# Two-layer mixture of experts on one core: whole expert products, other tile addresses, a rearranged router tail and a loop in another place

## The chip, the cores and the metric

One core of a Trainium2 chip runs the kernel. The metric is the device time of one execution in microseconds (us). The engines are TensorE (PE, with PEld for its weight loads), VectorE (DVE), ScalarE (ACT), GpSimd (POOL) and SyncE (SP, which issues the transfers). The line numbers (L911) are those of the kernel before.

## The reference

All is float32, 512 tokens of width 1024. Two layers of one kind come first, then a third block of another kind and a feed-forward layer. A layer of the first kind is

```python
h = rmsnorm(x, g_mix[i]);  u = h @ w_in[i]
...
x = x + merged @ w_o[i]
x = x + hierarchical_moe(rmsnorm(x, g_ffn[i]), ...)
ple_gate = jax.nn.sigmoid(rmsnorm(x, g_ple[i]) @ w_ple_gate[i])
x = x + (p[i] @ w_ple[i]) * ple_gate
```

with `merged` from a stick-breaking and a differential attention. The mixture has 4 groups of 8 experts. A token takes the best group by its group logits and in it the best 2 experts; each expert is `(silu(x @ w_gate) * (x @ w_up)) @ w_down` with a hidden width of 256, and its rows are weighted by the token's gates and added up. The third block has a dilated window attention, a gated linear recurrence and a block-sparse attention with a relative bias.

## The kernel before, in words

**Products.** Most float32 matmuls are made of three with rounded operands: an operand is split in a high part (`copyH`, L227 on ACT) and a low rest (`subL`, L240 on DVE or POOL), and `mm3` (L272 to L274) multiplies high by high, high by low and low by high. In the trace "out<-a,b" of a matmul names the moving operand a first and the stationary operand b second: `mm<-f,wh` is the feature-major projection `proj_f`, 512 columns of f against a 128x128 piece of a weight tile wh; `mm<-wh,q` is `add_out` (L639), the output projection, with 256 weight columns moving; `proj_v` (L484) has 256 weight columns moving too. Weights come by SP into `raw` tiles (4 of 4 KB per partition) and are cut into `wh` tiles (6). Tiles of one tag share a ring of buffers; `q` has 12, `o` 8, and `tmp`, `g`, `f16` belong to the phase "mix" (7, 4 and 2 buffers), `X`, `wu`, `gs`, `hid`, `y` and another `g` (4) to the phase "moe", whose memory is the same.

**Router.** `add_out` adds an output tile to x (L651) by 256 columns c and 128 tokens tt and calls `router.then(c, tt)`. That queues a transpose of x (L755), its split in high and low (L760 on ACT, L761 on DVE) and the products with the router's weights. Behind the last c of a token tile it forms the norm at once: a square on ACT (L333), the reciprocal root on DVE (L310 to L318), a scaled copy of 128x1024 on DVE (L345), the high part on ACT and the low part of 128x1024 on POOL (L240). These eight tiles `hs` fill the `o` ring. `moe_route` copies the logits (L808 on ACT), transposes them (L811) and runs the routing chain on DVE, from L814 to L903: best group, best two experts, gates, each token's place in the sorted rows.

**Experts.** The sorted rows stand in 17 groups g of two experts with 64 rows each (the last one has one). Tokens are gathered by products with one-hot tiles (`gather_oh`, L993 and L994 on DVE; `gather_rows` on PE, copied to X by ACT and DVE in turn). The up product multiplies 64 rows of two experts side by side, in the two halves of the array's columns: 8 pairs of matmuls of 64 stationary and 512 moving columns (`mm<-wu,X` and the same with raw, wh or q in place of wu). The down product has 4 pairs (`z<-wh,hid`, `z<-raw,hid`). Between them lie `gate`, `hidden` (transposes L1056), `rows` (the split of the result), `back` (transposes of the one-hot tile, L1036) and `combine` (`o<-q,g`, added to x by L1078 on DVE). An order written out by hand, for PE, ACT, DVE and POOL, interleaves all this: a list of steps, each one pair of matmuls of a product, and tables (`GAT`, `BAT`, `CAT`, `HT`) that say between which steps the other work goes. A weight's buffer is loaded again when the step that reads it last has been written.

**Ahead and behind.** A loop (`moe_overflow`, L1200 and L1202) for experts with more than 64 rows stands between the routing chain and the first gather. Its trip count is read from memory by every engine; with the inputs here it makes no turn, and all engines meet at it. Behind the steps the last groups' rows are combined (`z<-q,g`, added by L1179). Then come the norm of the next part and the p input's product: `ple_rows` (transposes L1289, `mm<-wh,o`, copies L1303) and the gate product. Outside the hand-written order a scheduler picks instructions by priority, so parts of `ple_rows` run among the last steps. Its tiles (p, its transposes and its results) are from the `o` ring too.

Of the kernel before, what the change touches and what calls it, by code (L numbers as in the profile page):

```python
# [18 lines left out]
S, D = 512, 1024  # L19
# [88 lines left out]
class Kern:  # L108
    def __init__(self, ctx, tc, A, out, dbg=None, stop=None):
# [7 lines left out]
        self.ph = None  # L117
# [4 lines left out]
    PHASES = {"mix": dict(tmp=7, g=4, f16=2, reset=1), "moe": dict(y=1, gs=2, g=4, X=2, hid=2, wu=NWU)}  # L122

    def phase(self, name):
# [6 lines left out]
        self.phbufs = dict(self.PHASES[name])  # L131

    def ring(self, tag, shape, dt):

        return self.t(tag, shape, dt, bufs={"raw": RAW, "wh": WHL}[tag])
# [106 lines left out]
    def wload(self, src, a, b, eH="act", eL="dve"):  # L242
# [4 lines left out]
        return self.wcut(raw, a, b, eH, eL)  # L247
# [5 lines left out]
    def wcut(self, raw, a, b, eH="act", eL="dve"):  # L253

        h, l = (self.ring("wh", [128, a, b], F32R) for _ in range(2))
# [236 lines left out]
    def proj_f_halves(self, hT, w, c0, r):  # L492

        r += [self.mmps([128, S]) for _ in range(2)]
        wc = [self.wload(self.wk(w, c0, kh), 4, 256) for kh in range(2)]
# [230 lines left out]
    def router(self, l, xs):  # L726
# [18 lines left out]
        self.routed = lt, r, hs  # L745
# [23 lines left out]
        def then(c, tt):  # L769
# [18 lines left out]
        return then  # L788

    def moe_route(self, l, xs):  # L790
# [3 lines left out]
        lt, r, hs = self.routed  # L794
# [13 lines left out]
        nc.scalar.copy(ls, lt)  # L808
# [94 lines left out]
        v.tensor_sub(GHL[:, :, 1], d, GHL[:, :, 0].bitcast(F32))  # L903
# [4 lines left out]
    def moe(self, l, xs):  # L908
# [9 lines left out]
        for g, tags in ((0, ("raw", "raw", "wh", "wh")), (1, ("q",) * 4)):  # L918
            for c in range(4):
                for i in range(2):  # L920
                    t = self.t(tags[c], [128, 2, 2, 256], F32, bufs={"raw": RAW, "wh": WHL, "q": 12}[tags[c]])
# [936 lines left out]
```

## Time and profile before

| | |
|---|---|
| median of 3 runs | 2855.8 us (2852.76 to 2857.8) |
| the profiled execution | 2855.61 us, span 2853.9 us |
| PE, PEld busy | 2691.7 (94%), 1995.1 (70%) |
| DVE, ACT, POOL busy | 1379.6 (48%), 973.3 (34%), 313.8 (11%) |
| DMA | 383.56 MB, 134 GB/s in the mean |
| granted clock of PE, mean | 0.968 |

The span is the time from the first to the last instruction; some 2 us lie around it. The expert stages are 504 to 845 us in the first layer and 1408 to 1751 us in the second. A row of a timeline has the start, the duration, engine, line, operation and tiles, and behind "x" how many were put together; where several stand in a row the duration goes to the end of the last. PE's ends are modelled and overlap the next start, so the pace of matmuls is read from start to start.

### The profile page before, as it was taken

To read this page: it belongs to the slowest core of one execution; us is meant where nothing else is said; L and a number is where in the kernel's file an instruction comes from. 1 tells how busy PE (TensorE), PEld (TensorE's weight loads), DVE (VectorE), ACT (ScalarE), POOL (GpSimd) and SP (SyncE) were. 2 spreads that over 40 slices of the span, in tenths; PEclk is the share of its full clock that TensorE was granted. 3 is DMA by queue.
4 is the path that set the end of the run, shared out by engine and by line. 5 is a ranking of instruction groups with operands and counts; after the bars stand their busy time and mean duration, and the time that the engine had idled before them with its cause. 6 is when DMAs were issued, how large, how long until landed. Compare 5 with 4: busy or idle time off the path is not lost.

```text
span 2853.9 us, 37149 instructions
## 1 busy us (share of the span) xinstructions
PE 2691.7 (94%) x14711; PEld 1995.1 (70%) x14711; DVE 1379.6 (48%) x2585; ACT 973.3 (34%) x1756; POOL 313.8 (11%) x346
## 2 busy tenths in 40 slices
PE   7899996999999989999699999899999899999998
PEld 6777785544548777788444545878776677877798
DVE  6677536233247567643633335754345812533323
ACT  4555322111124455532211113544453532322222
POOL 0221001000000022010100000210001533011101
PEclk9999997999999989999799999999999999999999
DMA  5112234788853211233778883322212233223322
GB/s 171 45 45 67 84 119 149 287 304 292 289 203 98 77 52 47 65 92 116 238 290 283 290 308 104 111 82 64 65 51 70 77 104 108 86 92 96 96 86 71
DMA packets 224770, 383.56 MB, mean 134 GB/s; under 512 B 19658, under 2 KB 162599, under 8 KB 224592
## 3 DMA queue, kind: packets, MB, share of 16 engines
q1 hardware_dynamic: 224592, 381.13, 39.8%
q8 instruction: 118, 1.93, 0.3%
q14 instruction: 60, 0.49, 0.1%
HBM read 374.23 MB, written 6.85 MB: 134 GB/s over the span
## 4 chain that ended last, share of the span: by engine, by line
PE 43%; DVE 5%; ACT 1%; POOL 1%; issue 1%; POOLq 0%; DVEq 0%; ACTq 0%
PE mm L272 8%; PE mm L274 8%; PE mm L273 7%; PE z L911 5%; PE mm L911 4%; PE o L911 2%; PE z L272 1%; PE z L274 1%; PE z L273 1%; DVE tmp L345 1%; PE o L524 1%; PE o L1440 1%; PE mm L484 0%; DVE tmp L1606 0%; PE z L1429 0%
## 5 line engine op out<-in xcount | busy, mean ns | idle before, releaser
L240 DVE TENSOR_TENSOR wh<-raw,wh 128x1024 fp32r<-128x1024 f32 (+1 forms) x251 | 304.1, 1214 | 474.2 <-ACT wh L227 471.9
L272 PE MATMUL mm<-f,wh 128*128 128x512 f32 x1296 | 519.0, 402 | 5.1 <-DVE q L238 2.3
L273 PE MATMUL mm<-f,wh 128*128 128x512 f32 x1296 | 518.8, 400 | 0.0
L274 PE MATMUL mm<-f,wh 128*128 128x512 f32 x1296 | 517.6, 400 | 0.1
L227 ACT ACTIVATE wh<-raw 128x1024 fp32r<-128x1024 f32 (+1 forms) x278 | 290.4, 1046 | 485.3 <-PE mm L273 331.8
L272 PEld LDWEIGHTS mm<-f,wh 128*128 128x128 f32 x1296 | 244.6, 189 | 71.1 <-issue 6.8
L274 PEld LDWEIGHTS mm<-f,wh 128*128 128x128 f32 x1296 | 244.9, 189 | 57.7 <-issue 2.1
L273 PEld LDWEIGHTS mm<-f,wh 128*128 128x128 f32 x1296 | 245.1, 189 | 55.5 <-issue 1.7
L911 PE MATMUL mm<-wu,X 128*64 128x512 f32 x928 | 229.2, 606 | 0.0
L911 PEld LDWEIGHTS z<-g,o 128*128 128x128 f32 x1152 | 141.6, 193 | 51.0 <-issue 14.6
L911 PE MATMUL z<-g,o 128*128 128x256 f32 (+1 forms) x1152 | 154.7, 289 | 10.8 <-DVE g L994 10.8
L911 PEld LDWEIGHTS o<-q,g 128*128 128x128 f32 x448 | 75.4, 188 | 104.4 <-issue 56.8
L484 PE MATMUL mm<-wh,f 128*128 128x256 f32 x960 | 138.4, 298 | 5.4 <-ACT f L386 3.1
L911 PE MATMUL o<-q,g 128*128 128x512 f32 x448 | 134.7, 422 | 3.3 <-DVE q L1078 3.3
L484 PEld LDWEIGHTS mm<-wh,f 128*128 128x128 f32 x960 | 128.1, 201 | 10.9 <-ACT f L386 4.8
L1078 DVE TENSOR_TENSOR q<-q,o 128x512 f32<-128x512 f32 x112 | 76.6, 684 | 108.7 <-PE o L911 108.7
L911 PEld LDWEIGHTS mm<-wu,X 128*64 128x64 f32 x928 | 55.5, 136 | 87.3 <-issue 79.2
L272 PE MATMUL mm<-wh,q 128*128 128x256 f32 x384 | 112.1, 292 | 3.7 <-ACT q L227 3.7
L274 PE MATMUL mm<-wh,q 128*128 128x256 f32 x384 | 110.1, 287 | 2.4 <-POOL q L240 2.2
L273 PE MATMUL mm<-wh,q 128*128 128x256 f32 x384 | 109.4, 285 | 0.0
L524 PE MATMUL o<-tmp,q 128*128 128x256 f32 x576 | 103.9, 319 | 1.6 <-DVE tmp L240 1.4
L524 PEld LDWEIGHTS o<-tmp,q 128*128 128x128 f32 x576 | 88.2, 217 | 15.1 <-ACT tmp L227 9.3
(436 smaller groups left out, 4610.8 us busy)
## 6 DMA issues: line engine op xcount, KB each, us to landing
raw<-in_w_in_dram SPq DMA_DIRECT2D x142, 512.0 KB, 3.5
wu<-in_w_exp_gate_dram SPq DMA_DIRECT2D x116, 512.0 KB
wu<-in_w_exp_up_dram SPq DMA_DIRECT2D x116, 512.0 KB, 8.0
wh<-in_w_exp_down_dram SPq DMA_DIRECT2D x76, 512.0 KB, 6.4
raw<-in_w_exp_down_dram SPq DMA_DIRECT2D x56, 512.0 KB, 6.0
raw<-in_w_gu_dram SPq DMA_DIRECT2D x44, 512.0 KB, 3.5
raw<-in_w_down_dram SPq DMA_DIRECT2D x20, 512.0 KB, 3.4
raw<-in_w_o_dram SPq DMA_DIRECT2D x16, 512.0 KB, 4.8
```

Source lines behind the costliest of these rows:

```text
L227: nc.scalar.activation(o, i, AF.Copy, scale=scale)
L240: e.tensor_sub(o, i, h)
L272: mm(ps, aH, bH, start=first, stop=False, skip_group_check=True)
L273: mm(ps, aH, bL, start=False, stop=False, skip_group_check=True)
L274: mm(ps, aL, bH, start=False, stop=last, skip_group_check=True)
L345: self.nc.vector.scalar_tensor_tensor(h.rearrange("t k p -> t p k"), x.rearrange("t (p k) -> t p k", k=8), r, gb.rearrange("t (p k) -> t p ...
L484: self.nc.tensor.matmul(ps[:, t], hT[k // 4][:, x, k % 4, sl], wc[k // 4][y][:, k % 4], start=t + x + y + k == 0, stop=x == 1 and k == 7, ...
L524: self.nc.tensor.matmul(po, v[kt // 2][:, x, kt % 2, vc], w[y][:, kt, :], start=x + y + kt == 0, stop=y == 1 and kt == nk - 1, skip_group_ ...
L911: mm = lambda *a, **k: nc.tensor.matmul(*a, **k, skip_group_check=True)
L1078: return lambda: v.tensor_add(xs[tt][:, cs], xs[tt][:, cs], po)
L1440: nc.tensor.matmul(po[:, m, qt % 2], v[:, qt - prev + j, vc], pT[:, m, j], start=m == 0 and j == 0 and qt % 2 == 0, stop=j == prev, skip_g ...
```

## The change

- The steps of the hand-written order are whole products: one step is a whole up or down product, its pairs back to back. Gathers, gates, backs, combines and hidden transposes go between the steps. Copies run right behind their matmuls. Gathered rows are copied by ACT alone. There are five one-hot tiles in place of four and six `wu` buffers in place of five.
- Before some rings a pad of unused bytes is allocated (one small memset on POOL each), the wh ring's tiles are 4608 bytes, and weights that move 256 wide start 64 bytes into theirs (`skip=64`).
- The router's norm is made from 128x256 pieces: POOL multiplies x by the gain into a transposed order, ACT squares, DVE forms the sum and the root. High and low of the first two token tiles are formed at once, on ACT and DVE; of the last two the high parts come behind the copy of the logits and the low parts behind the routing chain's last instruction.
- The loop for crowded experts stands behind the final combine.
- The scratch for transfer descriptors has 1024 bytes in place of 16384.

```diff
-RAW, WHL, NWU = 4, 6, 5
-HT = 4
+RAW, WHL, NWU = 4, 6, 6
 LM, LH, LF = 1, 1, 3
-
-GAT = (-25, -24, -23, -22, -9, -15, -13, -11, -9)
-BAT = (-7, -5)
-CAT = (40, 2)
...
+    def ring(self, tag, shape, dt, skip=0):
+
+        if tag == "raw":
+            return self.t(tag, shape, dt, bufs=RAW)
+        o = skip // 4
+        t = self.t(tag, [128, 1152], dt, bufs=WHL)[:, o:o + int(np.prod(shape[1:]))]
+        return t if len(shape) == 2 else t.rearrange({3: "p (a b) -> p a b", 4: "p (a b c) -> p a b c"}[len(shape)],
+                                                     **dict(zip("ab", shape[1:-1])))
...
+    PADS = {("sb", "q"): 320, ("sb", "raw"): 192, ("mix", "tmp"): 64, ("mix", "f16"): 256, ("mix", "g"): 320, ("moe", "g"): 128}
...
+        pad = self.PADS.get((self.phname if tag in self.phbufs else "sb", tag), 0)
+        if pad and (tag in self.phbufs, tag) not in self.padded:
+            self.padded.add((tag in self.phbufs, tag))
+            pool = self.phsb if tag in self.phbufs else self.sb
+            self.nc.gpsimd.memset(pool.tile([128, pad // 4], F32, name=f"pad_{self.n}")[:, 0:1], 0.0)
...
-        wc = [self.wload(self.wk(w, cols, kh), 4, 256) for kh in range(2)]
+        wc = [self.wload(self.wk(w, cols, kh), 4, 256, skip=64) for kh in range(2)]
...
+        ss = self.t("ss", [128, 4, 4], bufs=1)
+        xg = [self.F4([128, 8, 128]) for _ in range(4)]
+        self.routed = lt, r, hs, xg
...
-                todo.sort(key=lambda x: -x[0])
-                todo.pop()[1]()
-            if c == 3:
-                h = self.norm(xs[tt], gb, out=r[:, tt:tt + 1])
-                while tt == 3 and todo:
+                while todo:
                     todo.sort(key=lambda x: -x[0])
                     todo.pop()[1]()
-                o = [self.F4([128, 8, 128], F32R, "o") for _ in range(2)]
-                self.copyH(o[0], h, "act")
-                self.subL(o[1], h, o[0], "pool")
-                hs.append(o)
+            cs = slice(c * 256, c * 256 + 256)
+            turned = lambda a: a.rearrange("t (p k) -> t p k", k=8)
+            nc.gpsimd.tensor_mul(xg[tt][:, :, c * 32:c * 32 + 32].rearrange("t k p -> t p k"), turned(xs[tt][:, cs]),
+                                 turned(gb[:, cs]))
+            self.squares(xs[tt], c, ss[:, tt, c:c + 1])
+            if c == 3:
+                s = self.small([128, 1])
+                nc.vector.reduce_sum(s, ss[:, tt], axis=AX.X)
+                self.rstd(s, D, r[:, tt:tt + 1])
+                hs.append([self.F4([128, 8, 128], F32R, "o") for _ in range(2)])
+                if tt < 2:
+                    self.copyH(hs[tt][0], xg[tt], "act", r[:, tt:tt + 1])
+                    self.subL(hs[tt][1], xg[tt], hs[tt][0], "dve", r[:, tt:tt + 1])
...
-        nc.scalar.copy(ls, lt)
+        first = nc.scalar.copy(ls, lt)
+        for tt in (2, 3):
+            self.after(nc.scalar.activation(hs[tt][0], xg[tt], AF.Copy, scale=r[:, tt:tt + 1]), first)
...
-        v.tensor_sub(GHL[:, :, 1], d, GHL[:, :, 0].bitcast(F32))
+        last = v.tensor_sub(GHL[:, :, 1], d, GHL[:, :, 0].bitcast(F32))
+        for tt in (2, 3):
+            self.after(v.scalar_tensor_tensor(hs[tt][1], xg[tt], r[:, tt:tt + 1], hs[tt][0].bitcast(F32), op0=OP.mult,
+                                              op1=OP.subtract), last)
...
-                steps += [("up", g, j) for j in range(4 * ne(g))]
+                steps.append(("up", g))
             if g > 0:
                 if g == NG:
-                    steps += [None] * 2
+                    steps.append(None)
                 dn[g - 1] = len(steps)
-                steps += [("dn", g - 1, j) for j in range(2 * ne(g - 1))]
+                steps.append(("dn", g - 1))
...
-                free = up[g] + (4 * h + 3 if ne(g) == 2 else 2 * h + 1)
-                loads.setdefault(free, []).append(load_in)
+                loads.setdefault((up[g], 4 * h + 3), []).append(load_in)
...
-            return lambda: self.copyH(Xs[u][:, kk * 2:kk * 2 + 2, 0:n], pz[:, :, 0:n], "act" if kk % 2 == 0 else "dve")
+            return lambda: nc.scalar.copy(Xs[u][:, kk * 2:kk * 2 + 2, 0:n], pz[:, :, 0:n])
...
+                pa, X = self.mmps([128, 2, 256]), Xs[g // 2]
+                PS["a", g] = pa
+                n = 4 * ne(g)
+                for j in range(n):
+                    for i in range(2):
+                        k, e = (j, i) if two else (2 * j + i, 0)
+                        x0 = (g % 2 * 2 + e) * 64
+                        mm(pa[64 * i:64 * i + 64], X[:, k, x0:x0 + 64], IN.pop((g, e, k)), start=j == 0, stop=j == n - 1)
+                    for f in loads.pop((s, k), ()):
+                        f()
+                if two:
+                    gate(g, 0)
+                    gate(g, 1)
+                else:
+                    at(s + 1, lambda: folded("a", g, pa.rearrange("p j c -> p (j c)"), lambda: (gate(g, 0), gate(g, 1))))
+                at(max(s + 2, dn[g] - 1) + (not two), lambda: hidden(g))
...
+        for u in range(1, 9):
+            at(max(4 * u - 3, 1), lambda u=u: gather_gates(u))
+        def back_rows(y):
+            for j in range(7):
+                for x in range(4):
+                    at(min(4 * j + 6 + x, N), lambda j=j, x=x: combine((2 * j, 2 * j + 1), x, y))
+        back_rows(0)
+        for u in range(9):
+            for x in range(4):
+                if u:
+                    at(max(4 * u - 4 + x, 1), lambda u=u, x=x: gather_rows(u, x))
+                if x < 2 and 2 * u + x < NG:
+                    at(max(4 * u - 2 + x, 1 + x), lambda u=u, x=x: back(u, x))
+        back_rows(1)
...
+                at(4 * u - 6 + tt // 2, lambda u=u, tt=tt: gather_oh(u, tt))
...
-        self.moe_overflow(l, xs, hs, G, it, oe)
...
                 v.tensor_add(xs[tt], xs[tt], po[tt - t0].rearrange("p h c -> p (h c)"))
+        self.moe_overflow(l, xs, hs, G, it, oe)
         self.phase("mix")
...
-    nc = _bacc.Bacc("TRN2", target_bir_lowering=False, num_devices=1)
+    nc = _bacc.Bacc("TRN2", target_bir_lowering=False, num_devices=1, dynamic_dma_scratch_size=1024)
```

## Rows read from the trace of the kernel before

**Rows 1.** The page's part 1, busy us (share of the span) xinstructions.

```profile
PE 2691.7 (94%) x14711; PEld 1995.1 (70%) x14711; DVE 1379.6 (48%) x2585; ACT 973.3 (34%) x1756; POOL 313.8 (11%) x346
```

**Rows 2.** Busy time by stretch: PE, PEld, DVE, ACT, POOL, PEclk, DMA share, GB/s.

```profile
504.00:834.00 330.00, 330.00 (x1662) 160.83 (x1663) 111.10 (x236) 47.11 (x81) 0.00 (x0) 1.00 0.78 279
845.00:861.00 16.00, 16.00 (x70) 11.71 (x69) 10.54 (x14) 6.02 (x12) 1.05 (x2) 1.00 0.68 231
1371.00:1397.00 26.00, 4.35 (x26) 2.86 (x26) 22.65 (x73) 5.11 (x10) 7.06 (x3) 0.51 0.59 193
```

**Rows 3.** PE's timeline, 706 to 713 us, first layer's expert stage.

```profile
706.32 1.94 PE L911 MATMUL mm<-wu,X 128*64 128x512 f32 x8
708.19 1.19 PE L911 MATMUL o<-q,g 128*128 128x512 f32 x4
709.31 1.94 PE L911 MATMUL mm<-wu,X 128*64 128x512 f32 x8
...
712.32 1.08 PE L911 MATMUL z<-wh,hid 128*64 128x512 f32 x4
```

**Rows 4.** PE's timelines: first and last of the first layer's 114 narrow runs.

```profile
504.27 1.94 PE L911 MATMUL mm<-raw,X 128*64 128x512 f32 x8
...
843.12 1.94 PE L911 MATMUL z<-raw,hid 128*64 128x512 f32 x8
```

**Rows 5.** PE's timeline, 953.7 to 957 us, a 512-wide projection.

```profile
953.93 0.39 PE L272 MATMUL mm<-f,wh 128*128 128x512 f32 x1
...
956.96 0.39 PE L273 MATMUL mm<-f,wh 128*128 128x512 f32 x1
```

**Rows 6.** PE's timeline, 861 to 864 us, the p input's product.

```profile
861.16 0.39 PE L274 MATMUL mm<-wh,o 128*128 128x512 f32 x1
...
863.43 0.40 PE L272 MATMUL mm<-wh,o 128*128 128x512 f32 x1
```

**Rows 7.** Groups of PE instructions by form: xcount | busy us, mean ns.

```profile
L272 PE MATMUL mm<-f,wh 128*128 128x512 f32 x1296 | 519.0, 402 | 5.1 <-DVE q L238 2.3 <-ACT g L431 1.8 <-DVE tmp L1734 0.7
...
L272 PE MATMUL mm<-wh,q 128*128 128x256 f32 x384 | 112.1, 292 | 3.7 <-ACT q L227 3.7
...
L272 PE MATMUL z<-wh,q 128*128 128x256 f32 x96 | 27.2, 283 | 0.0
...
L272 PE MATMUL z<-wh,g 128*128 128x256 f32 x48 | 13.2, 276 | 0.0
```

**Rows 8.** Timeline of all engines, 1366 to 1397 us, second layer's router tail.

```profile
1366.38 0.28 PE L274 MATMUL mm<-wh,q 128*128 128x256 f32 x1
...
1370.56 0.42 DVE L651 SCALAR_TENSOR_TENSOR q<-mm,q 128x256 f32<-128x256 f32 x1
...
1374.02 1.97 DVE L345 SCALAR_TENSOR_TENSOR tmp<-q,small,tmp 128x1024 f32<-128x1024 f32 x1
...
1377.21 2.35 POOL L240 TENSOR_TENSOR o<-tmp,o 128x1024 fp32r<-128x1024 f32 x1 [3.44 <-ACT o L227]
1377.23 2.35 DVE L314 SCALAR_TENSOR_TENSOR small<-small,small 128x1 f32<-128x1 f32 x1
...
1377.87 0.58 ACT L808 COPY tmp<-o 36x512 f32<-36x512 f32 x1 [0.74 <-PE o L274]
...
1382.07 0.29 DVE L814 TENSOR_TENSOR g<-mm,small 128x144 f32<-128x144 f32 x1
...
1394.03 0.17 DVE L903 TENSOR_TENSOR ghl<-g,ghl 128x12 fp32r<-128x12 f32 x1
...
1396.22 0.62 DVE L993 TENSOR_SCALAR g<-c_all,gates 128x256 fp32r<-128x256 f32 x2 [2.02 <-issue]
```

**Rows 9.** DVE's timeline, 858 to 862 us, the first layer's final adds.

```profile
858.67 2.35 DVE L1179 TENSOR_TENSOR q<-q,z 128x1024 f32<-128x1024 f32 x2 [3.61 <-PE z L911]
```

**Rows 10.** DMA issues: xcount, KB each, us from issue to landing.

```profile
raw<-in_w_in_dram SPq DMA_DIRECT2D x142, 512.0 KB, 3.5
...
tmp<-in_g_mix_dram SPq DMA_DIRECT2D x3, 512.0 KB, 6.8
```

More of the change, by code (lines that the diff above doesn't have):

```diff
@@ L240, in subL, with wload @@
             e.tensor_sub(o, i, h)
-    def wload(self, src, a, b, eH="act", eL="dve"):
+    def wload(self, src, a, b, eH="act", eL="dve", skip=0):
         raw = self.ring("raw", [128, a, b], F32)
@@ L246, in wload, with wcut @@
             self.nc.sync.dma_start(raw if d is None else raw[:, :, d], ap)
-        return self.wcut(raw, a, b, eH, eL)
+        return self.wcut(raw, a, b, eH, eL, skip)
     def early(self, what):
         return self.tc.high_priority(EARLY[what])
-    def wcut(self, raw, a, b, eH="act", eL="dve"):
-        h, l = (self.ring("wh", [128, a, b], F32R) for _ in range(2))
+    def wcut(self, raw, a, b, eH="act", eL="dve", skip=0):
+        h, l = (self.ring("wh", [128, a, b], F32R, skip) for _ in range(2))
         with self.early("cut"):
@@ L494, in proj_f_halves @@
         r += [self.mmps([128, S]) for _ in range(2)]
-        wc = [self.wload(self.wk(w, c0, kh), 4, 256) for kh in range(2)]
+        wc = [self.wload(self.wk(w, c0, kh), 4, 256, skip=64) for kh in range(2)]
         for half in range(2):
@@ L793, in moe_route @@
         v = nc.vector
-        lt, r, hs = self.routed
+        lt, r, hs, xg = self.routed
         R = self.F4([128, 1024], tag="g")
@@ L920, in moe @@
                 for i in range(2):
-                    t = self.t(tags[c], [128, 2, 2, 256], F32, bufs={"raw": RAW, "wh": WHL, "q": 12}[tags[c]])
+                    t = self.F4([128, 2, 2, 256], tag="q") if tags[c] == "q" else self.ring(tags[c], [128, 2, 2, 256], F32)
                     for j, w in enumerate((wg, wu)):
@@ L971, in load_out @@
                 nout[0] += 1
-                t = OUT[g, i, k] = self.t(tag, [128, 1024], F32, bufs={"raw": RAW, "wh": WHL}[tag])
+                t = OUT[g, i, k] = self.ring(tag, [128, 1024], F32)
                 nc.sync.dma_start(t, weights(g, i)[2][k * 128:k * 128 + 128])
-                loads.setdefault(dn[g] + (2 * k + 1 if ne(g) == 2 else 1), []).append(load_out)
+                loads.setdefault((dn[g], 2 * k + 1), []).append(load_out)
         self.phase("moe")
@@ L1095, in work @@
         def work(s):
[L1097 removed]
+            kind, g = steps[s]
             two = ne(g) == 2
             if kind == "up":
[L1100 to L1129 removed]
@@ L1130, in work @@
-            for f in loads.pop(s, ()):
-                f()
+                pa, X = self.mmps([128, 2, 256]), Xs[g // 2]
[8 more added lines that the diff above has]
+                        f()
@@ new lines, in work @@
+                if two:
[4 more added lines that the diff above has]
+                at(max(s + 2, dn[g] - 1) + (not two), lambda: hidden(g))
+            else:
+                py = PS["y", g] = self.pst("z", [128, 1024], 2)
+                n = 2 * ne(g)
+                for j in range(n):
+                    for i in range(2):
+                        k, q, e = (j // 2, j % 2, i) if two else (i, j, 0)
+                        cs = slice(q * 512, q * 512 + 512)
+                        mm(py[64 * i:64 * i + 64, cs], HID[g][:, k, 64 * e:64 * e + 64], OUT[g, e, k][:, cs],
+                           start=k == 0 or not two, stop=k == 1 or not two)
+                    for f in loads.pop((s, j), ()):
+                        f()
+                if two:
+                    rows(g, 0)
+                    rows(g, 1)
+                else:
+                    at(s + 1, lambda: folded("y", g, py, lambda: (rows(g, 0), rows(g, 1))))
@@ L1156, in moe @@
         self.moe_blocks(oe, it)
+        for k in (3, 7):
+            loads.setdefault((0, k), []).extend([load_out] * 4)
         ET = mybir.EngineType
@@ L1162, in moe @@
                     if callable(f):
-                        at(s + 1, f)
-                if s in (3, 7) and s < N:
-                    for _ in range(4):
-                        loads.setdefault(s, []).append(load_out)
+                        f()
                 if s < N and steps[s]:
@@ L1311, in ple @@
         for c in range(4):
-            wc = [self.wload(self.wk(A["w_ple_gate"][l], c * 256, kh), 4, 256) for kh in range(2)]
+            wc = [self.wload(self.wk(A["w_ple_gate"][l], c * 256, kh), 4, 256, skip=64) for kh in range(2)]
             for tt in range(4):
```

52 lines of the change are left out of this document (5 added, 47 removed).

## The prediction, before the changed kernel was run

> **What bounds the kernel now.** I read the page's busy times first: TensorE (PE) is busy for 2691.7 us, 94% of the span [rows 1]. So the time falls if a matmul gets shorter, or if one of the gaps in which PE has nothing to do closes. The table by stretch shows where each applies. In the first layer's expert stage (504 to 834 us) PE is busy for all of 330 us at a granted clock of 1.00, while DMA moves 279 GB/s at a share of 0.78 [rows 2]: PE sets the pace and DMA stands close behind. In the router's tail (1371 to 1397 in the second layer) PE is busy for 4.35 us of 26 and DVE for 22.65: a vector chain sets the time [rows 2]. I then read start-to-start times in PE's timeline, because a busy time overlaps the next matmul's and hides the small costs. Last came the tail's timeline over all engines.
>
> **Part 1, runs.** A 64-column product is two matmuls side by side, and one with the same moving operand follows at once. Eight records start at 706.32 and the next full-width matmul at 708.19; four take 1.08 us busy where eight take 1.94 [rows 3]. So a pair costs (1.94 - 1.08) / 2 = 0.43 us. One whole cycle, eight narrow records and four 512-wide ones, goes from 706.32 to 709.31, 2.99 us [rows 3]. The work alone is 4 x 0.43 + 4 x 0.233 (the pace of a full matmul, below) = 2.65. The rest, 0.34 us, is the price of going to the narrow shape and back. The first layer has 114 runs of narrow products from 504.27 to 843.12 [rows 4], mostly of eight and of four records. After the change a product runs whole: 17 up products and 17 down products make 34 runs. That removes 80 switches, 80 x 0.34 = 27 us per layer, and 54 in both. Nothing hides it, since PE is never idle there. What now stands between the products must be ready in time: gate work on ACT and DVE has a whole down product (8 pairs, 3.4 us) as cover, and a combine's add lies behind four gather rows, so I charge nothing. If that cover fails, some 0.5 us per group come back, 17 x 0.5 = 8 us per layer at worst; the price of a switch itself I take as certain to a tenth. Bounds: 40 to 60 us of gain. The transfers must go faster: the same bytes in 303 us instead of 330 are 279 x 330 / 303 = 304 GB/s, a share of 0.85. The sixth weight buffer helps that, and I take it as possible.
>
> **Part 2, placement.** The trace of before has no run with other addresses, so I compare matmuls whose operands happen to lie differently, by the addresses at which the program of before puts its tiles. The 512-wide projection (moving tile f starts 64 bytes past a multiple of 128, weights on a multiple) starts 13 times from 953.93 to 956.96, every 0.233 us [rows 5]. The 512-wide product of the p input (both on a multiple) starts 10 times from 861.16 to 863.43, every 0.227 [rows 6]. At 256 columns it is the other way: z from wh and q (same offset) takes 283 ns in the mean, z from wh and g (different offset) 276 [rows 7]. The pads and the skip of 64 make the first kind alike and the second kind different. So 3 x 1296 = 3888 projections [rows 7] save 6 ns each, 24 us. The 3 x 384 of the output projection [rows 7], 7 ns each at most, save 8 us; I take 5, as PE waits in that stage too. z from wh and q saves 288 x 7 ns = 2 us, and the 512-wide combine and gather-like products some 5; about 2 go the other way where tiles meet differently than before. Sum -34 us. Bounds: nothing at one end, -40 at the other. I stay near the upper value since two widths agree with it in opposite directions. The pads' small memsets on POOL lie under other work. The other uses of the wider wh ring cost nothing I can find: the number of instructions is the same.
> The Trainium skill speaks against this part: its page "TensorE: Matmul & The Clock Gate", Part 2, step 1, says that PE has two independent SBUF read ports, so that loading the next weights takes no read bandwidth from the running matmul. By that, addresses should not matter, this part would be worth 0 instead of -34, and rows 5 and 6 would need another cause.
>
> **Part 3, the router's tail.** In the second layer the last output matmul starts at 1366.38 and DVE adds its result only at 1370.56, 3.9 us after its end, because strided products and reciprocal steps stand ahead of it on DVE [rows 8]. One such product takes 1.97 us (1374.02), and a 0.2 us step takes 2.35 (1377.23) while POOL's 2.35 us subtraction runs beside it (1377.21) [rows 8]. The copy of the logits follows at 1377.87, 6.9 us after the add, and the chain's first operation at 1382.07; the chain ends at 1394.20, and the first one-hot tile is begun at 1396.22, behind the loop's barrier [rows 8]. After the change the norm per tile is one POOL product and one ACT square per 256 columns. Its DVE part is short, POOL's 128x1024 subtraction is gone, and the last two roundings are ordered behind. Terms: the late add -3.6; between add and copy one strided product and one stalled step, -3.8; between copy and chain the same, -2.6; a stalled step in the chain -2.0; the barrier -2.0; the two low roundings ahead of the one-hot tiles, near a 1024-wide DVE addition (2.35 for two [rows 9]), +2.4. Sum -11.6 per layer, -23 for both. Bounds -14 to -26: the new POOL products (16 per layer, a quarter of 2.35 us each by size, up to all of it by stride) may stall DVE in their turn, which is the low end. On POOL itself up to 38 us lie beside PE's output projection, whose logits don't wait for them.
>
> **Part 4, the loop behind the rest.** Before, the final combine (845 to 861) has PE busy for all of 16.00 us [rows 2], because the p input's products fill its gaps, and the final adds end at 861.0 [rows 9]. Behind the loop, all that needs the buffers of hs or of the expert phase waits for its barrier: 2.0 us as in rows 8, then the landing of p and the gain, 3.5 (a weight tile) to 6.8 us (a gain tile) [rows 10]. SP's loads of p and gain are moved past the loop too; loads of other weights can still go ahead of it. Against it: PE loses about 5 us of fill ahead of the loop, so the combine ends earlier, and the products then fill the norm. I charge 2.0 + 5 + 4 of vector work (roundings of p and weights) - 5 = +6 per layer, +12 in both, bounds +4 to +24.
>
> **Sum.** -54 - 34 - 23 + 12 = -99, and I give back 5 for small stalls between whole products: -94. The profiled execution took 2855.61 us (span 2853.9) and stands 0.2 us below the median of 2855.8. So 2855.6 - 94 = 2762, rounded.
>
> **The rivals.**
> 1. Placement does nothing, or the offsets do not come out as read: 2762 + 34 = 2796. For it: rows 5 and 6 are different lines of the program, with different neighbours. Against it: the 256-wide ones show the reverse sign. Chance 0.18.
> 2. DMA becomes the bound in the expert stage: it stays at 279 GB/s, PE waits for weights at the head of each product, and the 54 us of the runs are lost: 2816. For it: a share of 0.78 already. Against it: not one wait of PE in 330 us. Chance 0.12.
> 3. Slower than before: the descriptor memory cut to a sixteenth makes transfers follow each other. One 512 KB tile in 3.5 us [rows 10] is 150 GB/s, so 279 x 330 = 92 MB would take 614 us, 311 more per layer: 3380. It decides against the change as soon as the rate falls below 92 MB / (303 + 47) = 263 GB/s, where 47 us twice eat the 94. Against it: the transfers come from SP's hardware queue in the page's rows [rows 10]. Chance 0.04.
> 4. The tail and the loop cancel and the runs are split by waits, so that little comes of parts 1, 3 and 4: about 2820, chance 0.04.
>
> **How the numbers follow.** Forecast 0.62, rivals 0.18, 0.12, 0.04, 0.04. The range goes from all good ends, -40 - 60 - 26 + 4 = -122 or 2734, up to rival 2, 2816. A measurement of this kernel tells 0.2%, 5.7 us, from no change. Only rival 3, and part of rival 4, are not faster: faster 0.94, same 0.02, slower 0.04.
>
> **What would show it.** In the changed profile: some 34 runs of narrow products per layer, of 32 and 16 records, and an expert stage of about 303 us without a wait of PE at a product's head; projections starting every 0.227 us; the add right after the last output matmul and the one-hot tiles some 12 us earlier; a gap of 6 to 9 us on PE behind the final adds. A projection still at 0.233 proves part 2 wrong, and a PE that waits for wu or raw tiles proves part 1 wrong.

## The result, and the profile after

The changed kernel takes 2806.5 us (median of 4 runs, 2804.2 to 2812.8) against 2856.4 of the kernel before beside it: a ratio of 0.9831, 95% interval 0.9812 to 0.9849. That is 50 us less, half of the 94 that were forecast and inside the range, which reaches up to 2816. The profiled executions have spans of 2853.9 and 2805.3, and their difference, -48.6, splits at events that both have (lengths in us, read from the timelines):

| stretch | before, layer 1 / 2 | after | change | forecast |
|---|---|---|---|---|
| router: last output matmul to first narrow product | 44.4 / 41.6 | 38.4 / 32.2 | -15.5 | -23 |
| experts: first to last narrow matmul | 340.2 / 341.3 | 321.4 / 319.3 | -40.8 | -54 |
| behind the experts: to the next 512-wide projection | 99.6 / 105.2 | 109.3 / 120.8 | +25.3 | +12 |
| all else: attention of layer 1 and 2, third block with feed-forward | 459.9 / 422.3, 999.4 | 459.3 / 418.1, 986.6 | -17.6 | -34 |

The busy times of the page answer to [rows 1]: PE has 65 us less to do, DVE 49.

```profile
PE 2627.0 (94%) x14711; PEld 2015.3 (72%) x14711; DVE 1331.0 (47%) x2557; ACT 999.2 (36%) x1840; POOL 329.6 (12%) x383
```

**Runs.** PE's timeline in the first layer's expert stage answers to [rows 3] (start, duration, engine, line, operation and tiles, count).

```profile
693.44 3.65 PE L933 MATMUL z<-wh,hid 128*64 128x512 f32 x16
...
702.29 7.09 PE L933 MATMUL mm<-wu,X 128*64 128x512 f32 x32
709.31 1.21 PE L933 MATMUL o<-q,g 128*128 128x512 f32 x4
```

A down product is now one run of 16 records and an up product one of 32 (half of that for the last group); between them stand gates, combines and gathers. The layer has 34 runs, as forecast, where it had 115 (the prediction counts 114).

**Stretches.** The table by stretch answers to [rows 2] (PE, PEld, DVE, ACT, POOL, granted clock, DMA share, GB/s).

```profile
504.00:815.00 311.00, 305.87 (x1655) 169.99 (x1652) 99.03 (x209) 57.65 (x100) 0.00 (x0) 1.00 0.78 289
816.00:820.00 4.00, 3.59 (x9) 0.77 (x8) 2.64 (x3) 1.22 (x2) 0.00 (x0) 0.50 0.29 94
833.00:842.00 9.00, 0.63 (x4) 0.34 (x3) 6.26 (x22) 4.26 (x8) 1.15 (x5) 0.74 0.54 178
841.00:847.00 6.00, 4.65 (x21) 4.30 (x22) 6.00 (x23) 1.07 (x4) 0.00 (x0) 0.50 0.08 33
1711.00:1724.00 13.00, 0.70 (x4) 0.23 (x2) 6.18 (x17) 4.26 (x8) 0.17 (x3) 0.64 0.50 164
```

PE is busy for 305.87 of 311 us in the expert stage: it has short waits that it had not before. The view of PE's waits in the first layer's whole stage (us in total, times, the longest) has no transfer in it; its two longest rows are

```profile
PE o L933 <- DVE q L1099: 2.7, 2, 1.9
PE z L933 <- ACT hid L1079: 1.1, 2, 0.7
```

DMA moves 289 GB/s where it moved 279, at the same share of 0.78. The stretches from 833 and from 1711 us, behind the final adds, hold almost no matmul, and the granted clock there is 0.74 and 0.64 in the mean. It is 0.50, the lower of its two levels (1.2 GHz), from 841 to 847 us, where PE begins again, and from 816 to 820, the end of the first layer's stage. There PE has just waited for DVE's adds (it is busy for 3.12 us of the 5 from 811 to 816), and the last down product's eight records take 3.68 us (from 816.46); the second layer's take 1.94 (from 1696.58) at a granted clock of 1.00.

**Pace.** 22 steps of the 512-wide projection in the third block, from start to start, answer to [rows 5]:

```profile
2063.82 0.39 PE L283 MATMUL mm<-f,wh 128*128 128x512 f32 x1
...
2068.81 0.39 PE L284 MATMUL mm<-f,wh 128*128 128x512 f32 x1
```

4.99 us for 22 are 227 ns, as forecast from [rows 6].

**Router.** The second layer's timeline answers to [rows 8].

```profile
1346.45 0.28 PE L284 MATMUL mm<-wh,q 128*128 128x256 f32 x1
...
1346.67 1.28 DVE L248 SCALAR_TENSOR_TENSOR o<-tmp,small,o 128x1024 fp32r<-128x1024 f32 x1 [0.35 <-ACT o L237]
...
1347.94 0.41 DVE L661 SCALAR_TENSOR_TENSOR q<-mm,q 128x256 f32<-128x256 f32 x1
...
1351.03 0.69 DVE L773 TENSOR_TENSOR f<-z,f 128x512 fp32r<-128x512 f32 x1
...
1352.58 0.58 ACT L825 COPY tmp<-o 36x512 f32<-36x512 f32 x1 [3.10 <-PE o L284]
...
1353.89 0.31 DVE L833 TENSOR_TENSOR g<-mm,small 128x144 f32<-128x144 f32 x1 [2.11 <-PE mm L830]
...
1363.89 2.47 DVE L924 SCALAR_TENSOR_TENSOR o<-tmp,small,o 128x1024 fp32r<-128x1024 f32 x2
1366.28 0.61 DVE L1014 TENSOR_SCALAR g<-c_all,gates 128x256 fp32r<-128x256 f32 x2
```

The add (1347.94) is 1.2 us behind the end of the last output matmul, not 3.9, and still late, since DVE is in the low rounding of an earlier token tile (1346.67, 1.28 us). The low part of the last turn (1351.03) is what the logits' copy at 1352.58 waits for, by way of the last products with the router's weights. From the end of the copy to the chain's first operation it is 0.7 us where it was 3.6. Behind the chain the two low roundings take 2.47 us to 1366.36, and the first one-hot tile is begun as they end.

**Router, first layer.** Here the same chain ends as early, but the gather does not follow:

```profile
473.72 0.31 SPq L1362 DMA_DIRECT2D tmp<-rel_dram  x1
...
476.63 0.17 DVE L922 TENSOR_TENSOR ghl<-g,ghl 128x12 fp32r<-128x12 f32 x1
...
480.00 2.28 PE L1372 MATMUL mm<-tmp,tmp 33*8 33x512 f32 x4 [6.99 <-DMA tmp<-rel_dram]
...
486.31 1.01 PE L933 MATMUL z<-g,o 128*128 128x256 f32 x3
```

The products for the relative bias (L1372) stand ahead of the gather on PE. Their table is asked for at 473.72 and they wait 6.99 us for it; the gather starts at 486.31, 9.5 us behind the chain. In the second layer it is 3.5. In the kernel before the same load was issued at 474.18, no earlier: there the chain ended at 487.78 only and covered it.

**Behind the experts.** The first layer's timeline, and then the second's (an SP row is the issue of a transfer):

```profile
832.44 2.35 DVE L1204 TENSOR_TENSOR q<-q,z 128x1024 f32<-128x1024 f32 x2 [4.02 <-PE z L933]
835.14 0.34 SPq L311 DMA_DIRECT2D tmp<-in_g_ple_dram  x1
835.17 1.06 ACT L343 ACTIVATE tmp<-q 128x1024 f32<-128x1024 f32 x1 [10.61 <-DVEq L1228]
...
839.58 1.96 DVE L355 SCALAR_TENSOR_TENSOR tmp<-q,small,tmp 128x1024 f32<-128x1024 f32 x1 [0.69 <-DMA tmp<-in_g_ple_dram]
...
841.69 0.66 PE L393 MATMUL z<-c_all,tmp 128*128 128x128 f32 x2 [8.37 <-DVE small L324]
```

```profile
1713.52 0.34 SPq L311 DMA_DIRECT2D tmp<-in_g_final_dram  x1
...
1713.91 0.60 SPq L311 DMA_DIRECT2D tmp<-in_g_mix_dram  x1
...
1714.57 0.94 SPq L311 DMA_DIRECT2D tmp<-in_g_ple_dram  x1
...
1722.03 1.96 DVE L355 SCALAR_TENSOR_TENSOR tmp<-q,small,tmp 128x1024 f32<-128x1024 f32 x1 [4.84 <-DMA tmp<-in_g_ple_dram]
...
1724.14 0.66 PE L393 MATMUL z<-c_all,tmp 128*128 128x128 f32 x2 [12.44 <-DVE small L324]
```

The loop itself costs 0.35 us from the end of the adds (834.79) to the first transfer. But the gain of the norm is asked for only then: it is used at 839.58 in the first layer and, third of three gains in the queue, at 1722.03 in the second. PE is idle for 8.4 and 12.4 us. The norm's squares stand behind the loop (L1228) as well: ACT is idle for 10.61 us until it and starts the first square at 835.17, though the first pair of adds was done at 828.42. With the loop in front (first experiment) the first square follows that pair's adds by 0.4 us.

### The profile page after: what moved, and what is told of

Read it like the earlier page. It is cut to its first block, busy times and chain, and to the rows that moved or that the text cites. A ratio compares the mean times of both kernels' runs of the same rounds, so it can differ in the third digit from the quotient of the medians.

```text
span 2805.3 us, 37258 instructions
## 1 busy us (share of the span) xinstructions
PE 2627.0 (94%) x14711; PEld 2015.3 (72%) x14711; DVE 1331.0 (47%) x2557; ACT 999.2 (36%) x1840; POOL 329.6 (12%) x383
## 5 line engine op out<-in xcount | busy, mean ns | idle before, releaser
L933 PE MATMUL mm<-wu,X 128*64 128x512 f32 x928 | 205.7, 595 | 0.0
L933 PEld LDWEIGHTS mm<-wu,X 128*64 128x64 f32 x928 | 64.0, 137 | 120.4 <-issue 117.7
L1069 DVE SCALAR_TENSOR_TENSOR gs<-gs,mm 128x256 f32<-128x256 f32 x32 | 13.5, 422 | 205.7 <-ACT gs L441 205.7
```

What stands on the lines that cost most here:

```text
L933: mm = lambda *a, **k: nc.tensor.matmul(*a, **k, skip_group_check=True)
L1069: v.scalar_tensor_tensor(sg[r], sg[r], 1.0, pa[r, 0], op0=OP.add, op1=OP.mult)
```

## The experiments

All but the seventh start from the changed kernel. Stretches are named as in the table above.

**The loop put back in front** of the first gather.

```diff
-        self.moe_overflow(l, xs, hs, G, it, oe)
         self.phase("mix")
...
+        self.moe_overflow(l, xs, hs, G, it, oe)
         for n in range(10):
```

> The changed kernel with the loop for crowded experts put back ahead of the first gather. Theory: behind the rest, the loop keeps the p input's work and the gain's load from running beside the final combine; from the last down product to the next layer's first 512-wide projection the changed kernel takes 109.3 and 120.8 us, 9.7 and 15.6 more than before. Back in front these stretches return to 100 and 105 us, the router's stretch gains the barrier's 2 us per layer, and the time falls by about 20 us, to 2786. Rival: the tail is long because the pads and the other order leave less to fill it with; then the tail stays within 3 us of 109 and 121 and the time rises by the barriers' 4 us, to 2810.

2788.2 us, ratio to before 0.9768 [0.9752, 0.9784]: 18 us faster than the change. Behind the experts 99.1 and 105.7 us, so -10.2 and -15.0; the router's stretch grows by 1.8 and 0.9. In the table by stretch the final combine and what follows are full of work again, at a granted clock of 0.97 to 1.00:

```profile
820.00:836.00 16.00, 15.85 (x65) 10.50 (x62) 8.45 (x12) 5.11 (x10) 1.28 (x5) 0.97 0.68 229
1710.00:1723.00 13.00, 11.77 (x60) 9.07 (x60) 10.44 (x33) 10.04 (x22) 0.00 (x0) 1.00 0.00 0
```

The theory holds. This version beats both kernels.

**The addresses put back.**

```diff
-    PADS = {("sb", "q"): 320, ("sb", "raw"): 192, ("mix", "tmp"): 64, ("mix", "f16"): 256, ("mix", "g"): 320, ("moe", "g"): 128}
+    PADS = {}
...
-        t = self.t(tag, [128, 1152], dt, bufs=WHL)[:, o:o + int(np.prod(shape[1:]))]
+        t = self.t(tag, [128, 1024], dt, bufs=WHL)[:, o:o + int(np.prod(shape[1:]))]
...
-        wc = [self.wload(self.wk(w, cols, kh), 4, 256, skip=64) for kh in range(2)]
+        wc = [self.wload(self.wk(w, cols, kh), 4, 256) for kh in range(2)]
```

> The changed kernel without the pads, without the skip and with wh tiles of 4096 bytes, so that the tiles lie otherwise than in the change. Theory: the 512-wide projection goes back from 227 to 233 ns from start to start, the 256-wide output projection from 114 to 120; in the hybrid and feed-forward part this costs 13 us, in the two attention parts, where other engines set the pace at times, 5 together, so the time rises by about 18 us, to 2824. Rival 1: addresses do not matter, the pace stays at 227 ns and the time within 3 us of 2806. Rival 2: every 512-wide projection counts in full, 24 us and more, 2832.

2820.4 us, ratio 0.9878 [0.9862, 0.9895], 14 us slower than the change. The same 22 steps take 5.13 us, 233 ns:

```profile
2067.47 0.40 PE L283 MATMUL mm<-f,wh 128*128 128x512 f32 x1
...
2072.60 0.40 PE L284 MATMUL mm<-f,wh 128*128 128x512 f32 x1
```

Of the 14, 12.0 are in the third block with the feed-forward; the second attention takes 2.9 more and the first 2.1 less, within what these scatter from kernel to kernel (next experiment). Rival 1 falls, and rival 2 too: the pace changes everywhere, the time clearly in one part. For the first attention one can see where the gain goes by sorting PE's start-to-start times: from before to after, those of up to 0.3 us sum to 366.0 and then 359.0 us, those between 0.3 and 0.6 to 50.9 and then 58.0 (139 and then 156 of them). What the faster matmuls give there comes back in short gaps; what PE waits for in them is not shown.

**The router put back:** the functions `router` and `moe_route` of before, whole, in the changed kernel.

```diff
-            self.squares(xs[tt], c, ss[:, tt, c:c + 1])
...
+                h = self.norm(xs[tt], gb, out=r[:, tt:tt + 1])
...
+                self.subL(o[1], h, o[0], "pool")
```

> The changed kernel with the router and the routing chain of before: the norm per token tile with a strided product on DVE, low parts on POOL, no roundings ordered behind the chain. Theory: from the last output matmul to the first narrow product the stretch grows from 38.4 and 32.2 us by the late add and the stalled steps, 2.7 + 2.7 + 3.0 + 2.0 less the two low roundings (2.5), some 8 us per layer; but in the first layer the products for the relative bias, which wait for their table until 480 us in the changed kernel because the four kept tiles hold their buffers, run earlier again, so there only 2 to 5. Time up by 10 to 13 us, to 2818. Rival: the new POOL products and squares cost as much as they save, time within 4 us of 2806.

2822.1 us, ratio 0.9883 [0.9866, 0.9899], 15.6 slower. The router's stretch is 42.0 and 39.7 us, so +3.6 and +7.5, 11 together as expected. The second layer's timeline shows the late add (4.1 us behind the last output matmul's end) and POOL's subtraction again:

```profile
1354.26 0.28 PE L284 MATMUL mm<-wh,q 128*128 128x256 f32 x1
...
1358.64 0.42 DVE L661 SCALAR_TENSOR_TENSOR q<-mm,q 128x256 f32<-128x256 f32 x1
...
1365.29 2.35 POOL L250 TENSOR_TENSOR o<-tmp,o 128x1024 fp32r<-128x1024 f32 x1 [3.44 <-ACT o L237]
...
1370.15 0.28 DVE L824 TENSOR_TENSOR g<-mm,small 128x144 f32<-128x144 f32 x1
```

Another 5.3 us are in the second attention, which is the same code. This stretch scatters: it took 418.1 us in the changed kernel, 423.2 with five buffers and 418.3 with the old steps. The cause of that stays open, and 5 us of a total in that stretch are not to be read as an effect.

**The steps put back:** the function `moe` of before with its tables, with five one-hot tiles, six buffers, the pads and the loop behind.

```diff
-                steps.append(("up", g))
+                steps += [("up", g, j) for j in range(4 * ne(g))]
...
+HT = 4
+GAT = (-25, -24, -23, -22, -9, -15, -13, -11, -9)
```

> The changed kernel with the order of before in the expert stage: steps of one pair, its tables of places, copies one step later, gathered rows copied by ACT and DVE in turn; five one-hot tiles and six weight buffers stay. Theory: the switches between narrow and full-width matmuls come back, 114 runs per layer in place of 34, and the stage from the first narrow product to the last down product goes from 321.4 and 319.3 us to about 340 each: time up by 40 us, to 2846. Rival: a good part of the 20 us per layer comes from the added buffers (weights wait less) or the addresses; then the stage stays below 333 us and the time below 2832.

2852.2 us, ratio 0.9990 [0.9981, 1.0000], 46 slower. The expert stage takes 341.6 us in both layers, +20.2 and +22.3; the third block 3.7 more, not explained. PE's timeline has the short runs of [rows 3] again:

```profile
705.08 1.19 PE L937 MATMUL o<-q,g 128*128 128x512 f32 x4
706.20 1.94 PE L937 MATMUL z<-wh,hid 128*64 128x512 f32 x8
707.97 1.03 PE L937 MATMUL mm<-wu,X 128*64 128x512 f32 x4
```

So the steps, with the places and engines of the copies that came back with them, make the whole gain of the stage, and the added buffers and the addresses none of it.

**One gain loaded first.**

```diff
+            gp = K.gbcast(A["g_ple"][l])
             if l == 0:
                 then = None
...
-            K.ple(l, xs, then)
+            K.ple(l, xs, then, gp)
```

> The changed kernel with one load moved: the gain of the p input's norm (g_ple) is fetched ahead of the two gains of the pair of norms that the second layer also needs there; the loop stays behind the rest. Theory: after the final adds the second layer waits 8.8 us for this gain since its load stands third behind the loop, where the first layer, whose load stands first, waits 4.8. With the load first, the wait in the second layer falls to about 5 us and the stretch from the last down product to the next 512-wide projection from 120.8 to about 117; the first layer stays at 109. Rival: the wait is the barrier's own or the falling clock's; then nothing moves by more than 1 us.

One execution, span 2800.5. In the second layer the wait for the gain is gone for the most part:

```profile
1710.69 0.34 SPq L311 DMA_DIRECT2D tmp<-in_g_ple_dram  x1
...
1714.92 1.96 DVE L355 SCALAR_TENSOR_TENSOR tmp<-q,small,tmp 128x1024 f32<-128x1024 f32 x1 [1.20 <-DMA tmp<-in_g_ple_dram]
```

From the end of the adds (1710.34) to the strided product it is 4.6 us where it was 8.9, and the stretch takes 116.3 us instead of 120.8. The first layer is the same (108.9). So the order of the queue is 4.4 of the second layer's 15.6.

**The relative tables behind the experts.**

```diff
-        if l == 0:
-            self.rel_tables()
         return hs, G, GHL, oe, it
...
         self.phase("mix")
+        if l == 0:
+            self.rel_tables()
```

> The changed kernel with the tables of the relative bias computed behind the first layer's experts instead of between its routing chain and its first gather. Theory: in the first layer the first gather waits for these products, whose table is loaded into a buffer that the kept tiles held until 473.7 us; without them the gather follows the chain by 3.5 us as in the second layer, not by 9.5, and the stretch from the last output matmul to the first narrow product falls from 38.4 to about 32; the tables find room in the idle time behind the final adds, so the total falls by 5 us or so. Rival: the gather waits for the low roundings and the one-hot tiles on DVE, and the stretch stays above 36.

One execution, span 2799.1, 6.2 less. The effect is as expected, though not for the reason that stands there: the kept tiles do not hold the load back, since its issue stands at 474.18 us in the kernel before and at 473.72 in the changed one, behind the experts' weights in SP's queue. It is the chain that now ends ahead of the load's landing. Without the tables the gather follows the chain's end (476.90) by 3.5 us, and the router's stretch takes 32.2 us:

```profile
476.73 0.17 DVE L922 TENSOR_TENSOR ghl<-g,ghl 128x12 fp32r<-128x12 f32 x1
...
480.36 1.31 PE L931 MATMUL z<-g,o 128*128 128x256 f32 x4 [7.25 <-DVE g L1013]
```

**The scratch alone,** in the kernel before.

```diff
-    nc = _bacc.Bacc("TRN2", target_bir_lowering=False, num_devices=1)
+    nc = _bacc.Bacc("TRN2", target_bir_lowering=False, num_devices=1, dynamic_dma_scratch_size=1024)
```

> The kernel before with nothing changed but the descriptors' scratch, 1024 bytes in place of 16384. Theory: all transfers here come from the hardware queue and their rate does not depend on it; span within 4 us of 2853.9 and 287 to 308 GB/s in the expert stages as before. Rival: a smaller scratch holds transfers back, and the expert stages or the span grow by more than 10 us.

One execution, span 2851.8, and the expert stage moves the 279 GB/s of [rows 2]. The forecast's rival 3 falls.

```profile
504.00:834.00 330.00, 330.00 (x1664) 161.09 (x1663) 111.00 (x235) 47.11 (x81) 0.00 (x0) 1.00 0.78 279
```

**Five buffers.**

```diff
-RAW, WHL, NWU = 4, 6, 6
+RAW, WHL, NWU = 4, 6, 5
```

> The changed kernel with five weight buffers for the up products instead of six. Theory: the expert stage of the changed kernel needs some 304 GB/s and DMA has little left, so with a buffer less the loads start later and PE waits at the head of some up products: 3 to 15 us more per layer than 321.4 and 319.3. Rival: the loads have enough room with five; the stages stay within 1 us.

The theory falls. One execution, 2808.5 us: the expert stages take 319.3 us each, DMA moves 289 GB/s, and no product waits for a weight. Five are enough.

```profile
504.00:812.00 308.00, 303.02 (x1643) 168.17 (x1643) 98.67 (x209) 56.57 (x98) 0.00 (x0) 1.00 0.79 289
```

**f moved up by 64 bytes.**

```diff
-    PADS = {("sb", "q"): 320, ("sb", "raw"): 192, ("mix", "tmp"): 64, ("mix", "f16"): 256, ("mix", "g"): 320, ("moe", "g"): 128}
+    PADS = {("sb", "q"): 320, ("sb", "raw"): 192, ("mix", "tmp"): 64, ("mix", "f16"): 320, ("mix", "g"): 256, ("moe", "g"): 128}
```

> The changed kernel with one pad moved: 64 bytes more ahead of the f tiles and 64 less ahead of the g tiles, so that of all tiles f alone starts elsewhere (64 bytes past a multiple of 128; the weights stay on one). Theory: the pace of a 512-wide matmul depends on whether its two operands start alike; the projections go from 227 back to 233 ns, the hybrid and feed-forward part from 986.6 to about 999, while the output projection (114 ns) and the stages of the experts stay; time about 2820. Rival: the pace comes from the wider wh ring or from the neighbours, and the projections stay at 227.

Neither held. 2810.0 us, ratio 0.9842 [0.9827, 0.9857], and 22 steps take 5.04 us, 229 ns:

```profile
2066.00 0.39 PE L283 MATMUL mm<-f,wh 128*128 128x512 f32 x1
...
2071.04 0.39 PE L284 MATMUL mm<-f,wh 128*128 128x512 f32 x1
```

Taken over all the projection's steps of up to 0.3 us the mean is 229.5. By addresses modulo 128 this run is like the kernel before; modulo 256 it is not: there f lay 64 and the weights 128 past a multiple, here f lies at 192. The next two runs ask which modulus counts.

**f moved down by 64, and up by 128.**

```diff
-    PADS = {("sb", "q"): 320, ("sb", "raw"): 192, ("mix", "tmp"): 64, ("mix", "f16"): 256, ("mix", "g"): 320, ("moe", "g"): 128}
+    PADS = {("sb", "q"): 320, ("sb", "raw"): 192, ("mix", "tmp"): 64, ("mix", "f16"): 192, ("mix", "g"): 384, ("moe", "g"): 128}
```

The second run has 384 and 192 in these two places.

> The changed kernel with 64 bytes less ahead of the f tiles and 64 more ahead of the g tiles: f starts 64 bytes past a multiple of 256 and the weights 128 past one, as in the kernel before; in the run with f moved the other way it started 192 past. Theory, formed from that run: the pace hangs on the distance from the weights to the moving operand modulo 256 bytes; 0 gives 227.9 ns, +64 gave 229.5, and the kernel before had -64 and 233.5. So here 233.5 ns, the hybrid and feed-forward part at 998 to 1000 us and the time near 2820. Rival: only whether the two start alike modulo 128 matters and the rest of that run's gain came from the wider ring; then 229.5 ns again, part at 989, time 2810.

> The changed kernel with 128 bytes more ahead of the f tiles and 128 less ahead of the g tiles: f starts on a multiple of 256, the weights 128 past one. Theory of the distance modulo 256: a fourth distance, no value known; if only equality counts, the projections take 229 to 234 ns and the hybrid and feed-forward part 989 to 1000 us. Rival, the rule of the prediction, that equality modulo 128 is enough: 227.9 ns and 986.6 us as in the changed kernel.

Down by 64: 2821.6 us, ratio 0.9879 [0.9863, 0.9896]; the third block with the feed-forward takes 998.4 us, and 22 steps 5.13:

```profile
2069.36 0.39 PE L283 MATMUL mm<-f,wh 128*128 128x512 f32 x1
...
2074.49 0.39 PE L284 MATMUL mm<-f,wh 128*128 128x512 f32 x1
```

Up by 128 (one execution, 2820.4 us): 998.4 us again, 22 steps 5.11:

```profile
2066.17 0.39 PE L283 MATMUL mm<-f,wh 128*128 128x512 f32 x1
...
2071.28 0.39 PE L284 MATMUL mm<-f,wh 128*128 128x512 f32 x1
```

The theory of the distance modulo 256 holds in the run that moves f down; equality modulo 128 is not enough.

**The loop in front and the tables behind.** The first and the sixth edit together.

> The changed kernel with the loop back in front of the first gather and the tables of the relative bias computed behind the first layer's experts. Theory: the two gains add up for the most part. The loop in front gave 18 us; in it the first gather of the first layer still comes 12.4 us after the routing chain, where the second layer has 5.1, so 7 us are to be had there, of which the tables' products take some 3 back in the stretch behind the experts, which is full of work now: about 2784 us. Rival: behind the experts the tables' loads and copies hold up the norm; 2788 as with the loop alone, or more.

2788.5 us, ratio 0.9764 [0.9750, 0.9777]: no faster than the loop in front alone. The rival is right. The first layer's router stretch does fall, from 40.2 to 35.6 us, but behind the experts it takes 107.9 us instead of 99.1, where the tables' products now stand between the adds and the p input's product on PE. And the gather still waits; the timeline names what ended the wait:

```profile
482.12 0.62 DVE L1012 TENSOR_SCALAR g<-c_all,gates 128x256 fp32r<-128x256 f32 x2 [3.59 <-DMA wh<-in_w_exp_down_dram]
...
483.18 1.19 PE L931 MATMUL z<-g,o 128*128 128x256 f32 x3 [10.83 <-DVE g L1013]
```

With the loop in front DVE stands idle for 3.59 us ahead of the first one-hot tile, and by the trace a weight's transfer ended that. In the first experiment this idle time is 8.95 us in the first layer, and by the trace SP at the loop (L1228) ended it, which had issued the tables' last transfers until 486.44 us. Whether the meeting point itself waits for transfers issued ahead of it was not tried.

## Why the prediction was right or wrong

The direction, the range and the order of the three gains held; each gain was taken too large and the cost too small. By parts, 13 + 16 + 7.5 + 13 us, less the 5 given back, make the 45 us between -94 and -48.6. That the time lies inside the range is partly luck: the range was drawn up to rival 2, and 2806.5 lies nearer to rival 2's 2816 and rival 1's 2796 than to 2762, though neither cause came about (the pace changed, and no product waits for a transfer). Rival 4 was half right: the router's 15.5 us and the 25.3 behind the experts more than cancel, but the runs were not split by waits. Put back one at a time, the steps, the router and the addresses are worth 46, 15.6 and 14 us, and the loop costs 18: about 57 together, with the 5 of the second attention among them, against the change's 50.

- **Part 1, runs: mechanism right, price mis-sized.** Forecast 80 switches x 0.34 = 27 per layer; the stage fell by 18.8 and 22.0, and putting the steps back cost 20.2 and 22.3. With each start-to-start time in the stage counted up to 0.6 us and no further, PE's work fell by 21.9 and 23.8 us, 0.27 to 0.30 per switch. The step that was mis-sized is the pair at 0.43 us, a difference of two busy times: in a whole product 16 pairs take 7.02 us (702.29 to 709.31), 0.44 each, and with that the cycle of [rows 3] leaves 0.30. On the other side what lies above 0.6 us grew by 3.1 and 1.8, which I had charged at nothing: two combines at the end of the stage wait 2.7 us for DVE's add, where no gather rows are left between them, and in the first layer the last down product then runs at the low granted clock (3.68 us in place of 1.94). Rival 2 was wrong: no product waits for a transfer, and with a buffer less nothing moved.
- **Part 2, placement: the pace right, the saving and the rule wrong.** The pace came out as worked (233 to 227, 120 to 115 ns). The step that failed is that 3888 projections save 6 ns each (23 us by that product, where the sum has 24): 1536 of them stand in the attention parts, of which the first takes as long as before, and the second scatters by more than they could give. The third block with the feed-forward gave 12.8 us for its 2352. The 5 us of the 512-wide combine did not come: `o<-q,g` has 233.1 ns from start to start before and 233.0 after. Of the small 256-wide groups z from wh and q went only from 120.0 to 117.8 ns, and z from wh and g from 113.3 up to 117.8. And that both operands on a multiple of 128 are alike was the wrong rule: with f up by 128 both still are, at 232.9 ns. The change gave the right pace since its pads make the distance zero modulo 256 too.
 The Trainium skill ("TensorE: Matmul & The Clock Gate", Part 2, step 1) says that loading weights takes no read bandwidth from the running matmul. The three runs that move f alone go against what I drew from it, that addresses should not matter: 227.9 to 233.5 ns by the address of one operand. They don't show the port at which the two meet.
- **Part 3, router: right in kind, too large by a third.** Second layer, forecast and measured: late add -3.6 and -2.7 (a low rounding of an earlier tile holds DVE for 1.28 us); from add to copy -3.8 and -2.7 (the roots of the last two tiles stand ahead of the turn on DVE); from copy to chain -2.6 and -2.9; in the chain -2.0 and -2.1; from chain to gather, barrier and low roundings together, +0.4 and +0.3. Then the way from the first one-hot tile to the first narrow product took 0.6 more. In the first layer what the longer chain had covered came out: the relative tables' load lands at 480.0 and their products run to 486.3, and the experiment without them gave 6 us back. I had taken the second layer's chain for both and had not asked what else must be done by its end.
- **Part 4, the loop: mechanism right, price mis-sized twice.** Behind the rest the barrier costs 0.35 us, not 2.0; in front (first experiment) the gather follows the second layer's chain by 5.1 us instead of 3.5, so there it is 1.6. The gain, forecast to land in 5, is used 4.4 us after its issue in the first layer and 7.5 in the second, where two other gains are ahead in the queue; I had counted no queue. And the overlap that was to give 5 back failed: the norm's squares wait for the loop too, and the product of the p input, which I let fill the norm, has its load asked for only at 835.53 and its first transposes at 842.14, behind the norm's first ones and at a granted clock of 0.50. Together +9.7 and +15.6 where +6 was forecast, and the loop in front gives 10.2 and 15.0 back.

## What to carry to other kernels

A faster matmul saves time only where PE sets the pace: sort the start-to-start times of a stretch before multiplying a gain by a count. A meeting point of all engines, even a loop of no turns, was cheap itself here (0.35 to 1.6 us) and dear by what could not start ahead of it (10 and 15 us); look for the loads behind it and their order in the queue. Where a chain gets shorter, ask what else must be done by its new end.

## What the runs showed of the hardware that was not expected

The pace of the 512-wide projection depends on the addresses of its operands modulo 256 bytes. Means of its start-to-start times of up to 0.3 us, some 3500 each, worked out from the runs' traces and the addresses of their programs, by the distance from the weights to f: 227.9 ns at 0 (the change), 229.5 at 64 (f moved up by 64), 232.9 at 128 (up by 128), 233.5 at 192 (the kernel before, the addresses put back, and f moved down by 64). In all of these the weights start 128 past a multiple of 256, so these runs alone do not tell the distance from f's own address.

The 256-wide products do, since there the same distance occurs at different addresses (means of times up to 0.15 us). At distance 0 the output projection before, with both operands at 128, takes 119.7 ns, and `proj_v` with f moved up by 64, both at 192, takes 119.7 too. At 64 `proj_v` takes 117.5 before (weights at 128, f at 64) and 117.4 after (192 and 128). At 192 the output projection after (128 and 192) takes 115.4 and `proj_v` with f up by 128 (192 and 0) 115.5. So it is the distance, and here its order is the reverse. Not every group follows: `z<-wh,q` has 117.8 ns at 192, `z<-wh,g` 113.3 at 64. All pieces of a weight tile lie alike modulo 256, so it is not shown whether the weights in use or those loaded meanwhile matter. Finer distances, and a larger modulus, were not tried.
